# One scan per pair in the state-space stage of a hybrid encoder layer, with norm work moved between ScalarE, GpSimd and VectorE

## The chip, the cores and the metric

The kernel runs on one core of one Trainium2 chip, as one launch. The metric is the device time in microseconds of that launch. Engines are called as in the profile: PE (TensorE), PEld (its weight loads), DVE (VectorE), ACT (ScalarE), POOL (GpSimd), SP (the queue that issues the transfers).

## The reference

One layer of a streaming encoder on 2048 prompt frames with 16 meta tokens in front and on 64 frames of a running stream, width 1024, all in FP32:

```python
z = rmsnorm(h, norm1_g) @ w_in                      # q (8 heads), k, v (2 heads), u (32 groups x 16 channels)
attn = windowed attention over 16 meta keys, the two chunks before and the own chunk, with a sink per head
# state-space model, per group g of 16 channels one complex diagonal state of 64:
bu = einsum(u, bb)                                  # bb, a from A, log_dt, B
x[t] = a * x[t-1] + bu[t]                           # x[-1] = 0 for the prompt, the cached state for the stream
y = Re(C x) + D u
zs = gelu(y);  s_out = zs * sigmoid(zs @ w_glu + b_glu)
h = h + concat(rmsnorm(attn), rmsnorm(s_out)) @ w_out
f = rmsnorm(h, norm2_g) @ w_up                      # 1024 -> 4096
h = h + square(relu(f)) @ w_down
```

Outputs are the frames of prompt and stream, the newest keys and values, and the last state (real and imaginary part) of prompt and stream.

## The kernel before

The 2128 frames are kept with channels in the rows. Matmuls of projections split each FP32 operand into a high and a low part (`xh`, `xl`; a cast on ACT, a difference on DVE) and add three products. The program runs in stages that overlap at their borders.

1. Input projection of u (`u_mm`, L825) and the preparation of the state-space tables on POOL; then the projections of q, k, v (L920) with the attention, chunk by chunk, the tables and maps of the state-space model beside them (`tables`, `store_g`, `store_k`), stored to `reca` and `recb` in DRAM.
2. The state-space stage. The 32 groups are taken as 16 pairs of groups. Frames are taken in 266 chunks of 8 (the last 8 chunks, from `PCH` = 258 on, are the stream's), so the recurrence over chunks has 266 steps. `ssm_step` runs for each pair: `ssm_in` (L1245) makes the input of the recurrence by a matmul, with real and imaginary part in the two halves of the rows and the two groups in two blocks; `ssm_align` (ACT, L1254) copies it so that the two groups lie in the two halves of the rows and the parts in two blocks; `ssm_mix` on DVE turns it by the phase tables (L1264 to L1268), scans (L1272), turns it back (L1276, L1277) and writes the states into `H` (L1282, L1285) with the parts in the rows again; `ssm_out` (L1294, L1295) makes y by two matmuls per group; `ssm_done` and `ssm_write` store it. `r8` holds one decay per row, `g0` the turned initial state. Two small copies take the last states into `fin` (L1287) and set the stream's initial state in `H` (L1288). Between the pairs stand the output projection's attention half (`out`, L1454, its sum on DVE in L1496) and the norms of the attention (`norm_square` to `norm_split`, one block of 352 frames at a time).
3. The GLU (`glu_mm`, L1672), the rest of the output projection into `hd` in DRAM, in six blocks of 352 frames; for the first two blocks the sums of squares for the MLP's norm are collected as the blocks come (`h_squares`).
4. The MLP in three blocks of 704 frames. Up and down projection are done by a seven-product scheme on 2 x 2 blocks (`product`, L1973; `unit`, L2068). Its left operands are combinations of four quarters of the normed frames: for the first block they are made by `x0_load`, `x0_gain`, `x0_sub`, `x0_cut` during the last two blocks of the output projection and after it; the products come in the order `ORD` = 1, 5, 6, 3, 7, 2, 4. The space of operands other than 1 and 6 is only free once the output projection is through.

A Newton step refines each reciprocal root that ACT makes as exp(-ln(v)/2) (`newton`, called by `rsqrt` and by the norms).

All instructions go through `Order.arrange`, a list scheduler written in the kernel: it estimates a length for each instruction, follows the dependences through tiles, pools and DRAM, ranks instructions by the longest way to the end, and fixes one order per engine. Any edit thus draws up every engine's order anew. Each engine and each queue then works in its order.

## Time and profile before

| | us |
|---|---|
| three runs, median (lowest to highest) | 2102.73 (2100.11 to 2104.24) |
| the profiled execution | 2103.09 |
| its span (first to last instruction) | 2100.5 |
| PE busy | 2003.0 (95%) |
| DVE busy | 1800.0 (86%) |
| ACT busy | 1221.7 (58%) |
| POOL busy | 397.0 (19%) |

The span is what the profiler sees between the first and the last instruction; the time of a run is a little longer. Busy time counts an engine's own instructions, overlaps once. The mean granted TensorE clock over the span was 0.984 of full speed.

### The profile page before, as it was taken

What the parts mean: (1) busy time and instruction counts of PE and PEld (TensorE: products, weight loads), DVE (VectorE), ACT (ScalarE), POOL (GpSimd) and SP (SyncE); (2) the same over time, 40 slices, a digit from 0 to 9 for tenths busy, and PEclk for the clock granted to TensorE, in tenths of its full rate; (3) what the DMA queues carried; (4) which work ended last, traced back from release to release, by engine and by line L of the source; (5) the groups of instructions that cost most, each with busy time, mean ns of one, the idle gap of its engine ahead of it and who ended that gap; (6) DMA issues with size and microseconds to landing.
All of it is one profiled execution on the core that took longest, in us unless ns stands there. A gap on an engine that the chain in (4) does not pass through costs nothing.

```text
span 2100.5 us, 34600 instructions
## 1 busy us (share of the span) xinstructions
PE 2003.0 (95%) x12100; PEld 1931.1 (92%) x12100; DVE 1800.0 (86%) x3315; ACT 1221.7 (58%) x2496; POOL 397.0 (19%) x525
## 2 busy tenths in 40 slices
PE   8989999997789988999999999999999999999999
PEld 8987888786679977999999999999999999999999
DVE  8958996679977778999999998789978977887778
ACT  6447677743255545655555666665656655566554
POOL 7954311000002052333233301000000100000000
PEclk9999999999899998999999999999999999999999
DMA  6532332467664385654666676556745764444432
GB/s 224 153 63 76 98 97 72 146 210 239 205 209 127 118 263 189 212 181 165 226 215 201 210 249 220 160 150 207 224 140 152 240 200 141 137 135 138 138 121 96
DMA packets 308335, 354.41 MB, mean 169 GB/s; under 512 B 28865, under 2 KB 220992, under 8 KB 307650
## 3 DMA queue, kind: packets, MB, share of 16 engines
q1 hardware_dynamic: 308018, 352.21, 53.8%
q8 instruction: 95, 1.56, 0.3%
q14 instruction: 78, 0.64, 0.1%
q10 hardware_dynamic: 144, 0.00, 0.0%
HBM read 260.15 MB, written 94.07 MB: 169 GB/s over the span
## 4 chain that ended last, share of the span: by engine, by line
PE 67%; DVE 19%; ACT 5%; DMA 5%; issue 3%; SPq 0%; POOL 0%; DVEq 0%; ACTq 0%; POOLq 0%
PE psd L2068 28%; PE bB L1973 10%; PE bA L1973 10%; PE bC L1973 8%; PE pso L1454 3%; PE psqkv L920 3%; PE psg L1672 2%; DMA hd<-xo 1%; PE pu L825 1%; DVE ul L1963 1%; DVE ab L1272 1%; DVE ss L799 1%; PE pv L1185 1%; DVE wl L2037 1%; DVE acc L2077 1%
## 5 line engine op out<-in xcount | busy, mean ns | idle before, releaser
L2068 PE MATMUL psd<-hh,wh 128*128 128x352 f32 x1344 | 433.8, 323 | 3.8 <-DVE acc L2077 2.9
L2068 PE MATMUL psd<-hl,wh 128*128 128x352 f32 x1344 | 432.0, 321 | 2.0 <-DVE hl L2056 2.0
L2068 PE MATMUL psd<-hh,wl 128*128 128x352 f32 x1344 | 430.6, 321 | 0.0
L2077 DVE TENSOR_TENSOR acc<-psd,acc 128x352 f32<-128x352 f32 x624 | 313.2, 514 | 36.5 <-PE psd L2068 35.7
L2068 PEld LDWEIGHTS psd<-hh,wh 128*128 128x128 f32 x1344 | 252.0, 188 | 6.2 <-DVE acc L2077 3.8
L2068 PEld LDWEIGHTS psd<-hl,wh 128*128 128x128 f32 x1344 | 252.7, 188 | 2.7 <-DVE hl L2056 2.6
L2068 PEld LDWEIGHTS psd<-hh,wl 128*128 128x128 f32 x1344 | 252.3, 188 | 0.0
L1962 ACT CAST uh<-ur 128x512 fp32r<-128x512 f32 x144 | 89.3, 620 | 151.3 <-PE bB L1973 64.0
L2037 DVE TENSOR_TENSOR wl<-d,wh 128x512 fp32r<-128x512 f32 x240 | 175.2, 730 | 0.3 <-ACT wh L2036 0.2
L2036 ACT CAST wh<-d 128x512 fp32r<-128x512 f32 x240 | 146.5, 617 | 34.1 <-PE psd L2068 28.3
L1973 PE MATMUL bA<-xl,uh 128*128 128x352 f32 x480 | 155.9, 325 | 5.4 <-DVE xl L1791 5.4
L1973 PE MATMUL bA<-xh,uh 128*128 128x352 f32 x480 | 157.6, 328 | 3.0 <-ACT xh L1790 1.6
L1962 ACT CAST uh<-us 128x512 fp32r<-128x512 f32 x128 | 79.4, 621 | 133.5 <-PE bB L1973 68.5
L1973 PE MATMUL bB<-xh,uh 128*128 128x352 f32 x480 | 156.0, 325 | 0.0
L1973 PE MATMUL bA<-xh,ul 128*128 128x352 f32 x480 | 155.9, 325 | 0.0
L1973 PE MATMUL bB<-xh,ul 128*128 128x352 f32 x480 | 155.4, 324 | 0.0
L1973 PE MATMUL bB<-xl,uh 128*128 128x352 f32 x480 | 154.8, 323 | 0.0
L920 PE MATMUL psqkv<-wqa,xh 128*128 128x384 f32 (+1 forms) x544 | 138.3, 348 | 7.0 <-ACT z L933 6.7
L1973 PE MATMUL bC<-xl,uh 128*128 128x352 f32 x384 | 125.4, 327 | 5.6 <-DVE xl L1791 5.6
L2056 DVE TENSOR_TENSOR hl<-hid,hh 128x352 fp32r<-128x352 f32 x240 | 129.2, 538 | 1.1 <-ACT hh L2055 1.1
L1963 DVE TENSOR_TENSOR ul<-ur,uh 128x512 fp32r<-128x512 f32 x144 | 108.7, 755 | 24.6 <-ACT uh L1962 24.6
L1973 PE MATMUL bC<-xh,ul 128*128 128x352 f32 x384 | 125.2, 326 | 2.3 <-DVE ul L1963 2.2
(446 smaller groups left out, 5295.7 us busy)
## 6 DMA issues: line engine op xcount, KB each, us to landing
ur<-in_w_up_dram SPq DMA_DIRECT2D x160, 256.0 KB
d<-in_w_down_dram SPq DMA_DIRECT2D x128, 256.0 KB
us<-usd SPq DMA_DIRECT2D x128, 256.0 KB
d<-dsd SPq DMA_DIRECT2D x96, 256.0 KB
hd<-xo SPq DMA_DIRECT2D x48, 352.0 KB
usd<-s SPq DMA_DIRECT2D x64, 256.0 KB
dsd<-d SPq DMA_DIRECT2D x48, 256.0 KB
dx<-in_w_down_dram SPq DMA_DIRECT2D x48, 256.0 KB
```

Of the source, the lines that this page charges most:

```text
L799: nc.vector.tensor_reduce(out=ss[b], in_=x.rearrange("p k n -> p n k"), axis=AX.X, op=ALU.add)
L920: nc.tensor.matmul(t["ps"][c][:n, :384], x, w[k][:, c * 384 : c * 384 + 384], start=(k == 0 and i == 0), stop=(k == KT - 1 and i == 2))
L1454: nc.tensor.matmul(ps, w, x, start=(i == 0), stop=(i == len(seq) - 1))
L1672: nc.tensor.matmul(ps, w[:, k, m * P : (m + 1) * P], x[:, k], start=(k == 0 and i == 0), stop=(k == 3 and i == 2))
L1962: nc.scalar.copy(h, src)
L1963: nc.vector.tensor_sub(l, src, f32(h))
L1973: nc.tensor.matmul(ps, w[:, k], x[:, k], start=(p in BANK and k == 0 and a == 0), stop=False, skip_group_check=True)
L2036: nc.scalar.copy(h, src)
L2037: (e if p in POOLED[i >= NPR] else v).tensor_sub(l, src, f32(h))
L2056: eng.tensor_sub(l, src, f32(h))
L2068: nc.tensor.matmul(ps, w[:, c], y, start=(p in DFIRST and n == 0), stop=False, skip_group_check=True)
L2077: v.tensor_add(ACC[eh, nh][:, x], ps, ACC[eh, nh][:, x])
```

## The change

It edits four things.

1. State-space stage. The scan of a pair is one instruction over both parts and over prompt and stream: its multiplier is a tile `dk` that ACT makes from a mask `dm` (ones, with zeros where a recurrence begins) and the decay, and the stream's turned initial state is added to its first step beforehand. `H` keeps the layout of the scan, groups in the rows and parts in the blocks, so two sums over all rows replace four over half the rows, and each of the two state matmuls of a pair becomes two over 64 rows; `recb` is stored to match. The small copies go from DVE to ACT. The last states are put in the output's order once, at the end (`ssm_last`).
2. `newton` makes the square of y on ACT first and is then two DVE operations instead of three.
3. The variance of the attention's, GLU's and MLP's norms (a scale and a shift of a PSUM row) goes from DVE to ACT.
4. From POOL to DVE: the sums of squares of the first two blocks, the products with the norm's root in `gain`, the differences in `x0_sub`, and the low part of operand 2 (`x0_rest`).

```diff
 def newton(y, v, t, eng):
-    eng.scalar_tensor_tensor(out=t, in0=v, scalar=-0.5, in1=y, op0=ALU.mult, op1=ALU.mult)
-    eng.tensor_mul(t, t, y)
+    nc.scalar.activation(t, y, AF.Square)
+    eng.scalar_tensor_tensor(out=t, in0=v, scalar=-0.5, in1=t, op0=ALU.mult, op1=ALU.mult)
     eng.scalar_tensor_tensor(out=y, in0=t, scalar=1.5, in1=y, op0=ALU.add, op1=ALU.mult)
...
             for c, t in enumerate((vr, vi)):
-                for gg in range(2):
-                    r = slice(64 * gg, 64 * gg + 64)
-                    nc.sync.dma_start(recb[js, 64 * c : 64 * c + 64, gg * P : (gg + 1) * P].rearrange("j p (d c) -> p j d c", c=16),
-                                      t[r, :, 1:9, :])
+                nc.sync.dma_start(recb[js, :, c * P : (c + 1) * P].rearrange("j p (d c) -> p j d c", c=16), t[:, :, 1:9, :])
...
-        elif i in (2, 3):
-            c = i - 2
-            for lo, hi, init in ((0, PCH, 0.0), (PCH, NCH, g0[:, c, j : j + 1])):
-                v.tensor_tensor_scan(out=x["ab"][:, c, lo:hi], data0=r8[:, j : j + 1].broadcast_to((P, hi - lo)),
-                                     data1=x["ab"][:, c, lo:hi], initial=init, op0=ALU.mult, op1=ALU.add)
+        elif i == 2:
+            x["dk"] = wide("dk")
+            nc.scalar.activation(x["dk"], Sx["dm"], AF.Copy, scale=r8[:, j : j + 1])
+            ab = x["ab"][:, :, PCH]
+            v.scalar_tensor_tensor(out=ab, in0=g0[:, :, j], scalar=r8[:, j : j + 1], in1=ab, op0=ALU.mult, op1=ALU.add)
+        elif i == 3:
+            fl = lambda a: a.rearrange("p c n -> p (c n)")
+            v.tensor_tensor_scan(out=fl(x["ab"]), data0=fl(x["dk"]), data1=fl(x["ab"]), initial=0.0, op0=ALU.mult, op1=ALU.add)
...
             H = x["H"] = GH[j % 2]
-            for gg in range(2):
-                r = slice(64 * gg, 64 * gg + 64)
-                v.tensor_sub(H[0:64, gg, 1:], x["p1"][r, 0], x["p2"][r, 1])
-            for gg in range(2):
-                r = slice(64 * gg, 64 * gg + 64)
-                v.tensor_add(H[64:, gg, 1:], x["p1"][r, 1], x["p2"][r, 0])
-            gs = slice(2 * j, 2 * j + 2)
-            v.tensor_copy(Sx["fin"][:, :, gs].rearrange("p q g -> p g q"), H[:, :, PCH : NCH + 1 : NCH - PCH])
-            v.tensor_copy(H[:, :, PCH], Sx["h0"][:, gs])
+            v.tensor_sub(H[:, 0, 1:], x["p1"][:, 0], x["p2"][:, 1])
+            v.tensor_add(H[:, 1, 1:], x["p1"][:, 1], x["p2"][:, 0])
+            nc.scalar.copy(Sx["fin"][:, :, :, j].rearrange("p q c -> p c q"), H[:, :, PCH : NCH + 1 : NCH - PCH])
+            nc.scalar.copy(H[:, :, PCH], Sx["h0"][:, :, j])
+
+    def ssm_last():
+        for c in range(2):
+            for gg in range(2):
+                nc.scalar.copy(Sx["st"][64 * c : 64 * c + 64, :, gg::2], Sx["fin"][64 * gg : 64 * gg + 64, :, c])
+        nc.sync.dma_start(O["st"], Sx["st"])
...
-            nc.tensor.matmul(y[:, gg, :NCH], x["rb"][:, gg * P : gg * P + P], x["H"][:, gg, 0:NCH], start=False, stop=True)
+            r = slice(64 * gg, 64 * gg + 64)
+            for c in range(2):
+                nc.tensor.matmul(y[:, gg, :NCH], x["rb"][r, c * P : c * P + P], x["H"][r, c, 0:NCH], start=False, stop=(c == 1))
...
-        nc.vector.tensor_scalar(out=v, in0=ps, scalar1=1.0 / 512, scalar2=EPS, op0=ALU.mult, op1=ALU.add)
+        nc.scalar.activation(v, ps, AF.Copy, scale=1.0 / 512, bias=EPS)
...
-                nc.gpsimd.tensor_add(HS[n], HS[n], sq[:, i])
+                nc.vector.tensor_add(HS[n], HS[n], sq[:, i])
...
-            nc.gpsimd.tensor_mul(x, x, M["rs"][:, nh].unsqueeze(1).broadcast_to((P, 2, OB)))
+            nc.vector.tensor_mul(x, x, M["rs"][:, nh].unsqueeze(1).broadcast_to((P, 2, OB)))
...
-        nc.vector.tensor_scalar(out=var, in0=ps, scalar1=1.0 / D, scalar2=EPS, op0=ALU.mult, op1=ALU.add)
+        nc.scalar.activation(var, ps, AF.Copy, scale=1.0 / D, bias=EPS)
...
-    out_block(NOB - 1, {0: (lambda: x0_sub("d", "b", "a", e), lambda: u_get(0, (0, 0), (1, 0))),
+    out_block(NOB - 1, {0: (lambda: x0_sub("d", "b", "a", v), lambda: u_get(0, (0, 0), (1, 0))),
...
-                        2: (lambda: x0_sub("b", "c", "b", e),), 3: (lambda: x0_sub("a", "c", "d", v),),
+                        2: (lambda: x0_sub("b", "c", "b", v),), 3: (lambda: x0_sub("a", "c", "d", v),),
...
-            x0_cut(2, "d", e)
+            x0_cut(2, "d", v)
```

What this makes of the engines' orders is shown at three places. First DVE in the middle of the state-space stage, one pair (`o` and `p` are the turned input and output, `ab` the scan's tile; scans read as SCALAR_TENSOR_TENSOR here). Before:

```order
L1267 TENSOR_TENSOR ab<-o_5589,o_5590 128x266
L1410 TENSOR_TENSOR ss<-sq 128x352
L1268 TENSOR_TENSOR ab<-o_5589,o_5590 128x266
L1282 TENSOR_TENSOR H_5195<-p_5594,p_5595 64x266 x2
L1285 TENSOR_TENSOR H_5195<-p_5594,p_5595 64x266 x2
L1272 SCALAR_TENSOR_TENSOR ab<-r_90,ab 128x258
L1287 COPY fin<-H_5195 128x2x2
L1272 SCALAR_TENSOR_TENSOR ab<-r_90,g_89,ab 128x8
L1288 COPY H_5195<-h_5190 128x2
L1272 SCALAR_TENSOR_TENSOR ab<-r_90,ab 128x258
L1272 SCALAR_TENSOR_TENSOR ab<-r_90,g_89,ab 128x8
```

These are ten operations on states and scan (two rows stand for two each). With the change the same place reads:

```order
L1269 TENSOR_TENSOR ab<-o_5586,o_5587 128x266
L1287 TENSOR_TENSOR H_5192<-p_5591,p_5592 128x266
L1288 TENSOR_TENSOR H_5192<-p_5591,p_5592 128x266
L1270 TENSOR_TENSOR ab<-o_5586,o_5587 128x266
L1507 TENSOR_TENSOR xo<-pso,xo 128x352
L1276 SCALAR_TENSOR_TENSOR ab<-g_89,r_90,ab 128x2
L1266 TENSOR_TENSOR o_5655<-RI,ra 128x532
L1279 SCALAR_TENSOR_TENSOR ab<-dk,ab 128x532
```

The ten operations became four (the sum `xo` of a projection and the first turn of the next pair now stand between them).

Then PE at the same place, from one pair's output to the next pair's input (`psy` the output y, `pss` the recurrence's input, `pso` the output projection). Before:

```order
L1294 MATMUL psy<-U,rb 128x266
L1245 MATMUL pss<-U,ra 128x266
L1295 MATMUL psy<-H_5195,rb 128x266
L1294 MATMUL psy<-U,rb 128x266
L1295 MATMUL psy<-H_5195,rb 128x266
```

Each group has one matmul on the states. With the change:

```order
L1303 MATMUL psy<-U,rb 128x266
L1306 MATMUL psy<-H_5190,rb 128x266 x2
L1303 MATMUL psy<-U,rb 128x266
L1306 MATMUL psy<-H_5190,rb 128x266 x2
L1247 MATMUL pss<-U,ra 128x266 x2
```

Each matmul on the states is there twice, over half the rows, and the full-row matmuls stand around each two of them.

Last, DVE from the last sums of the output projection to the MLP's first operands (`xa` to `xd` the four quarters of the normed frames, `rs` the norm's root, `xl` a low part). Before:

```order
L421 SCALAR_TENSOR_TENSOR rs<-ms,rs 128x352
L1496 TENSOR_TENSOR xo<-pso,xo 128x352 x3
L1791 TENSOR_TENSOR xl_8020<-xa,xh_8019 128x704
L1496 TENSOR_TENSOR xo<-pso,xo 128x352 x3
L1791 TENSOR_TENSOR xl_8020<-xa,xh_8019 128x704
L1496 TENSOR_TENSOR xo<-pso,xo 128x352
L1809 TENSOR_TENSOR xa<-xc,xd 128x704
L1791 TENSOR_TENSOR xl_8176<-xd,xh_8175 128x704
```

Only low parts and one pair of differences are DVE's here. With the change:

```order
L1820 TENSOR_TENSOR xd<-xb,xa 128x704
L1507 TENSOR_TENSOR xo<-pso,xo 128x352 x3
L1802 TENSOR_TENSOR xl_8021<-xa,xh_8020 128x704
L1793 TENSOR_TENSOR xc<-xc,rs 128x704 x2
L1820 TENSOR_TENSOR xb<-xc,xb 128x704 x2
L1974 TENSOR_TENSOR ul<-s,uh 128x512
L1820 TENSOR_TENSOR xa<-xc,xd 128x704
L1507 TENSOR_TENSOR xo<-pso,xo 128x352 x3
L1820 TENSOR_TENSOR xa<-xc,xd 128x704
L1802 TENSOR_TENSOR xl_8107<-xa,xh_8106 128x704
L1802 TENSOR_TENSOR xl_8177<-xd,xh_8176 128x704
```

The products with `rs` and the differences, which stood on POOL, now stand on DVE among the sums of the last projections. On PE the twelve matmuls of the first MLP product, which came after the last projection, now stand among the last 60 matmuls of it.

## Rows read from the trace of the kernel before

**Rows 1.** The page: busy us, share of the span, instructions.

```profile
PE 2003.0 (95%) x12100; PEld 1931.1 (92%) x12100; DVE 1800.0 (86%) x3315; ACT 1221.7 (58%) x2496; POOL 397.0 (19%) x525
```

**Rows 2.** Busy time by stretch: start:end, length, engines (instructions), granted clock, DMA share, GB/s.

```profile
455.00:590.00 135.00, 103.16 (x466) 84.75 (x467) 130.15 (x302) 44.61 (x94) 0.00 (x0) 0.91 0.73 234
640.00:740.00 100.00, 99.98 (x612) 98.34 (x611) 74.69 (x120) 53.04 (x86) 18.44 (x16) 1.00 0.44 132
767.00:830.00 63.00, 46.69 (x223) 41.76 (x223) 50.85 (x64) 31.44 (x60) 24.94 (x14) 0.81 0.58 191
1225.00:2075.00 850.00, 850.00 (x5322) 849.58 (x5321) 710.80 (x1382) 515.67 (x1041) 29.99 (x21) 1.00 0.54 168
```

**Rows 3.** Groups by line, PE, 455 to 590 us: instructions, busy us, mean ns, idle before.

```profile
L1454 PE MATMUL pso<-xh,zt 128*128 128x352 f32 x182 | 52.9, 357 | 0.5 <-ACT xh L1437 0.5
L1454 PE MATMUL pso<-xl,zt 128*128 128x352 f32 x92 | 32.3, 351 | 3.4 <-DVE xl L1438 3.4
...
L1295 PE MATMUL psy<-H,rb 128*128 128x266 f32 x60 | 21.5, 444 | 8.9 <-DVE H L1288 8.9
L1245 PE MATMUL pss<-U,ra 128*128 128x266 f32 x64 | 20.5, 439 | 16.4 <-DMA ra<-reca 14.5 <-DMA U<-ud 1.7 <-issue 0.2
```

**Rows 4.** Timeline of PE in the state-space stage: start us, us, instruction.

```profile
483.38 0.61 PE L1294 MATMUL psy<-U,rb 128*128 128x266 f32 x2
483.83 0.61 PE L1295 MATMUL psy<-H,rb 128*128 128x266 f32 x2
```

**Rows 5.** Groups by line, DVE, 455 to 590 us.

```profile
L1272 DVE TENSOR_TENSOR_SCAN ab<-r,ab 128x258 f32<-128x258 f32 x32 | 22.1, 690 | 0.4
L1282 DVE TENSOR_TENSOR H<-p,p 64x266 f32<-64x266 f32 x32 | 13.6, 424 | 0.6 <-PE psy L1295 0.4
...
L1272 DVE TENSOR_TENSOR_SCAN ab<-r,g,ab 128x8 f32<-128x8 f32 x32 | 6.9, 216 | 0.1
...
L1438 DVE TENSOR_TENSOR xl<-x,xh 128x704 fp32r<-128x704 f32 x6 | 5.3, 881 | 0.0
...
L1288 DVE COPY H<-h 128x2 f32<-128x2 f32 x15 | 2.3, 156 | 0.0
...
L1417 DVE TENSOR_SCALAR v<-psr 128x352 f32<-128x352 f32 x3 | 1.6, 517 | 0.0
```

**Rows 6.** Timeline of DVE in the state-space stage.

```profile
480.67 0.70 DVE L1272 TENSOR_TENSOR_SCAN ab<-r,ab 128x258 f32<-128x258 f32 x1
...
482.28 0.70 DVE L1264 TENSOR_TENSOR o<-RI,ra 128x532 f32<-128x532 f32 x1
```

**Rows 7.** Groups by line, whole span: the score matmuls on 128 and on 70 rows.

```profile
L1168 PE MATMUL s<-QT,KB 128*128 128x256 f32 x62 | 21.3, 348 | 2.9 <-ACT e L1176 2.3 <-DVE KB L1019 0.6
...
L1168 PE MATMUL s<-QS,KS 70*128 70x256 f32 x62 | 19.5, 323 | 1.9 <-DVE QS L1156 1.9
```

**Rows 8.** Timeline of PE where a 32-column operand follows a full one.

```profile
246.95 0.51 PE L920 MATMUL psqkv<-wqa,xl 128*128 128x384 f32 x2
247.39 0.41 PE L636 MATMUL pm<-vr,bd 128*32 128x128 f32 x2
```

**Rows 9.** Groups by line: POOL and DVE, 740 to 805 us; PE, 767 to 805 us.

```profile
L1809 POOL TENSOR_TENSOR xd<-xb,xa 128x704 f32<-128x704 f32 x2 | 4.0, 2023 | 0.0
...
L1791 DVE TENSOR_TENSOR xl<-xc,xh 128x704 fp32r<-128x704 f32 x2 | 3.2, 1622 | 0.0
L1791 DVE TENSOR_TENSOR xl<-xd,xh 128x704 fp32r<-128x704 f32 x2 | 3.2, 1616 | 0.0
L1809 DVE TENSOR_TENSOR xa<-xc,xd 128x704 f32<-128x704 f32 x2 | 2.9, 1426 | 0.0
...
L1973 PE MATMUL bA<-xl,uh 128*128 128x352 f32 x13 | 5.9, 454 | 5.4 <-DVE xl L1791 5.4
...
L1973 PE MATMUL bC<-xl,uh 128*128 128x352 f32 x8 | 3.9, 491 | 5.6 <-DVE xl L1791 5.6
```

More of the change, by code (lines that the diff above doesn't have):

```diff
@@ L1220, in ssm_open @@
         Sx["sp"] = ssp.enter_context(pool("sp", 1, "right"))
-        h0 = Sx["h0"] = Sx["sp"].tile([P, G], F32, name="h0")
-        nc.sync.dma_start(h0, I["h0"])
-        Sx["fin"] = Sx["sp"].tile([P, 2, G], F32, name="fin")
+        h0 = Sx["h0"] = Sx["sp"].tile([P, 2, PAIRS], F32, name="h0")
+        nc.sync.dma_start(h0, I["par"][:, 3:5])
+        dm = Sx["dm"] = Sx["sp"].tile([P, 2, NCH], F32, name="dm")
+        nc.gpsimd.memset(dm, 1.0)
+        nc.gpsimd.memset(dm[:, :, 0], 0.0)
+        nc.gpsimd.memset(dm[:, :, PCH], 0.0)
+        Sx["fin"] = Sx["sp"].tile([P, 2, 2, PAIRS], F32, name="fin")
+        Sx["st"] = Sx["sp"].tile([P, 2, G], F32, name="st")
         for i in range(2):
@@ L1625, in tile_trunk @@
     z_load(3)
-    nc.sync.dma_start(O["st"], Sx["fin"])
+    ssm_last()
     pys.close()
@@ L1647, in h_squares @@
             HS[n] = WO["na"].tile([P, OB], F32, tag=f"hs{n}", name="hs", bufs=1)
-            nc.gpsimd.tensor_add(HS[n], sq[:, 0], sq[:, 1])
+            nc.vector.tensor_add(HS[n], sq[:, 0], sq[:, 1])
         else:
             for i in range(2):
-                nc.gpsimd.tensor_add(HS[n], HS[n], sq[:, i])
+                nc.vector.tensor_add(HS[n], HS[n], sq[:, i])
     def glu_split(n, ks):
```

## The prediction

> **What bounds the kernel now.** I read the busy shares first [rows 1]: PE has work for 95% of the span, so most of this kernel is bound by matmuls, and an edit elsewhere pays only where PE waits. The busy time by stretch [rows 2] shows where that is. From 1225 to 2075 us PE is busy without a break, and its 5322 records give the pitch of a matmul of 352 columns at full clock: 850 / 5322 = 0.160 us. From 640 to 740 us it is full too. Two stretches differ. In the state-space stage, 455 to 590 us, PE is busy 103.16 of 135 us at a mean granted clock of 0.91, while DVE is busy 130.15 us: DVE is the bound. At the start of the MLP, 767 to 830 us, PE is busy 46.69 of 63 us at a clock of 0.81, DVE 50.85 us and POOL 24.94 us. The edits that matter fall into these two.
>
> What PE's work there would take at full clock is needed below. In the first stretch its 466 records are 182 + 92 = 274 output-projection matmuls [rows 3] and 192 others, nearly all halves of the FP32 matmuls of the state-space model (each such matmul leaves two records). Two halves follow two halves after 483.83 - 483.38 = 0.45 us [rows 4], 0.225 us each. So 274 x 0.160 + 192 x 0.225 = 43.8 + 43.2 = 87.0 us. In the second, 223 x 0.160 = 35.7 us of work stand in 63 us: 27.3 us are lost to waits and to the lower of the two clock levels (1.2 against 2.4 GHz).
>
> **State-space stage, what DVE sheds.** In each of 16 pairs the four scans go, two of 258 and two of 8 elements (0.690 and 0.216 us [rows 5]), with the two small copies between them: by their starts 482.28 - 480.67 = 1.61 us [rows 6]. The four 64-row sums into H go too, 4 x 0.424 = 1.70 us [rows 5]. In comes one scan of 532 elements. By the two lengths shown a scan costs (0.690 - 0.216) / 250 = 1.90 ns per element, so 0.216 + 524 x 0.0019 = 1.21 us. It reads a whole tensor as multiplier where the old one read one number per row, which no row shows; I take the old rate, as the nearest. Its ends: 0.5 us less per pair at the rate of the sums (0.424 us for 266 elements [rows 5]), 1.0 us more, 16 us in all, if the second stream doubles the old rate. Further come one two-element operation at 0.16 us, as the small copy, and two sums of 266 elements over all rows at no more than 0.42 us each, as the 64-row ones [rows 5]: 2.21 us in all. Net 1.61 + 1.70 - 2.21 = 1.10 us per pair, 17.6 us over 16.
>
> Three norms in this stage also lose the variance and one product of Newton's step to ACT: 3 x 2 x 0.517 [rows 5] = 3.1 us. DVE falls from 130.15 to about 109.5 us. The multiplier tile, the two small copies and Newton's square land on ACT: about 16 x 1.1 and 3 x 1 us, an estimate from DVE's small copy and from 532 elements at a bit over 1 ns each. ACT is busy 44.61 of 135 us [rows 2], so 65 us leave it free. The copy of the initial state now stands between H and the matmul that reads it, on another engine; where PE has no projection to run meanwhile that is some 0.4 us per pair, inside the allowance below.
>
> **State-space stage, what PE gains.** H now holds the real part in one block and the imaginary part in the other, the two groups in the two halves of the rows. So each of 32 matmuls on 128 rows becomes two on 64. Fewer rows do not shorten a matmul: the score matmul on 70 rows takes 0.323 us, the one on 128 rows 0.348 us [rows 7]. So 64 more halves at 0.225 us come on top: 14.4 us. With them come changes between full and 64-row operands, four per pair, 64 in all. No row shows that; nearest is the change to a 32-column operand: two matmuls of 384 columns (0.160 x 384 / 352 = 0.175 us each) begin at 246.95 us, and the next, of the other shape, at 247.39 instead of 247.30 [rows 8]: 0.1 us. 64 x 0.1 = 6.4 us. PE then needs 87.0 + 14.4 + 6.4 = 107.8 us, nearly the same as DVE.
>
> The Trainium skill (TensorEngine Tiling (Array Packing), Key Properties) says that a change of tiling mode drains TensorE, and also that different tiles may execute in parallel. The latter finds no use here: in the new order two neighbouring 64-row matmuls read the same rows. What the former would do is rival A.
>
> So the stage holds 109.5 us of DVE's and 107.8 us of PE's work, each in its own in-order queue. I add the 4.85 us for which DVE idles now (135 - 130.15 [rows 2]; the stage begins with a wait for tables, and PE waits 14.5 us for them in all [rows 3]), and 3 us because two full engines wait for each other at times, a third of what PE now waits for H, 8.9 us [rows 3]. That is 117 us, **18 us less**. Some projections that no longer fit into the stage run after it, in place of waits for transfers; I cost that at nothing, and 1 to 2 us if those waits are gone.
>
> **Start of the MLP.** Ten operations on the first operands (six products with the norm's root, four differences) and two low parts go from POOL to DVE. One takes 2.02 us on POOL [rows 9] and 0.88 us on DVE where POOL rests, as the low part of the same shape in [rows 5]. Beside a busy POOL, DVE's own operations of that shape take 1.62, 1.62 and 1.43 us on average, twice each [rows 9]: 2 x (0.74 + 0.74 + 0.55) = 4.1 us lost by these alone. So DVE takes on 12 x 0.88 = 10.6 us and gets back 4 to 8. What changes is the order: the products and differences now stand ahead of the last projections, where PE is busy, and POOL's serial chain (12 x 2 = 24 us) is off the path. PE's waits for a low part of x, 5.4 + 5.6 us [rows 9], mostly go. Late next are the two operands whose frames are loaded only once the last projections have freed their space: 4 us of wait are left for them. With a busier PE part of the low clock goes too: it hides up to 0.19 x 63 = 12 us [rows 2], I take 3. 11 - 4 + 3 = **10 us less**. Ends: 6 us worse (10.6 - 4, nothing hidden) to 22 us better (27.3 less a first wait of 5).
>
> **The rest.** Newton's squares, variances and 14 sums of squares (POOL to DVE) elsewhere lie beside a PE that is full (its second and last row) [rows 2] or, in the attention stage, are small: 1 us less in all, with 3 us either way, since every engine's order is drawn up anew. The states' rows and their one store at the stage's end are a few small copies, hidden by projections.
>
> Sum: 18 + 10 + 1 = 29 us. The profiled execution took 2103.1 us (span 2100.5, 2.6 around it), 0.4 above the median shown. 2103 - 29 = **2074 us**.
>
> **Rivals.**
> A. *The change of shape drains PE.* A drained change costs at most a matmul's length less its pitch, 0.444 - 0.225 = 0.22 us [rows 3, 4], and a weight load that is no longer hidden, 84.75 / 467 = 0.18 us [rows 2]: 0.40 us. 64 x 0.40 = 25.6 us put PE at 127 us and the stage, with 5 us of waits, at 132: 3 us gained, 2089 us. The page named above states the drain, without a price. For it: PE would be the bound at once. Against it: the 0.1 us of [rows 8]. Chance 0.13.
> B. *The MLP's start gains nothing.* DVE has 50.85 us of work in 63 and takes more into its in-order queue, where the sums of the projections wait behind it, and PE for their buffers. Then 18 + 1 us are left: 2084 us. Against it: the stretched rows. Chance 0.17.
> C. *Slower.* The drains of A keep the granted clock at its lower level through the stage, and a change costs twice as much, 0.8 us: PE needs 101.4 + 64 x 0.8 = 153 us, the stage with 5 us of waits 158. That is 23 us lost, 11 gained elsewhere: 2115 us. It decides from 0.68 us per change: 101.4 + 43.5 + 5 = 150 us, which eats the other 11 us and 4 more. Against it: the price is far above the one row there is. Chance 0.04.
> D. *A and B together*: 3 + 0 + 1 us, 2099 us. Chance 0.04.
>
> **Numbers.** The forecast has 0.62, with a range of its own from 2060 (24 + 16 + 3 less) to 2086 (12 + 5). The range to hold 8 times in 10 takes in A, B and the far ends: from 2057 (22 + 22 + 2 less) to 2091 (6 + 4 + 2). A measurement of this kernel tells about 0.2%, 4 us, from no change. Faster by more: the forecast, A and B, 0.92; within it: D, 0.04; slower: C, 0.04.
>
> **What would show it.** Right, if the state-space stage takes about 117 us, with one scan of 1.2 us per pair, DVE and PE both busy over 90% of it, the granted clock near 1 and 64-row halves at 0.225 us; and if the first MLP products stand among the last projections, with no wait of PE for a low part over 2 us. Wrong, if at each change of rows a matmul comes 0.4 us late (A), if the scan's rate is not 1.9 ns, if PE waits for the sums of the last projections (B), or if DVE waits for ACT's copies of the next pair, which I cost at nothing because in the new order they serve a pair three later.

## The result, and the profile after

| | before | after |
|---|---|---|
| median of the runs timed side by side, us (lowest to highest) | 2103.48 (2100.11 to 2105.42) | 2068.68 (2065.12 to 2071.01) |
| ratio, 95% interval | | 0.9835 (0.9822 to 0.9848) |
| span of the profiled execution, us | 2100.5 | 2067.8 |
| PE, DVE, ACT, POOL busy, us | [rows 1] | 2007.6, 1761.2, 1258.5, 355.3 |

34.8 us less; 2074 was forecast, in a range from 2057 to 2091. The sum is nearly right, but not all of its parts are. I cut both executions at the same five points of the program: the first matmul of the state-space stage (`pss`), the last matmul of y (`psy`), the last GLU matmul (`psg`), the first sum of a unit of the MLP (`acc` from `sa`) and the last sum. First the busy time by stretch of the kernel before, cut so (start:end, length, busy us and instructions of PE, PEld, DVE, ACT and POOL, granted clock, DMA share, GB/s):

```profile
0.00:456.10 456.10, 420.12 (x2514) 380.31 (x2515) 369.57 (x632) 285.93 (x652) 182.18 (x393) 0.99 0.42 120
456.10:593.50 137.40, 105.95 (x478) 86.79 (x479) 133.57 (x311) 44.61 (x94) 0.00 (x0) 0.91 0.72 229
593.50:729.30 135.80, 132.27 (x805) 129.43 (x804) 98.43 (x154) 82.84 (x124) 15.86 (x14) 1.00 0.47 146
729.30:828.80 99.50, 82.58 (x439) 76.39 (x438) 77.86 (x105) 48.82 (x90) 41.57 (x24) 0.88 0.70 225
828.80:2096.70 1267.90, 1262.06 (x7870) 1258.13 (x7868) 1120.07 (x2115) 759.54 (x1537) 157.43 (x94) 1.00 0.56 178
```

The same view of the changed kernel:

```profile
0.00:446.90 446.90, 415.43 (x2511) 381.55 (x2511) 359.41 (x604) 294.21 (x681) 175.93 (x396) 0.98 0.42 120
446.90:565.90 119.00, 117.22 (x535) 87.33 (x535) 109.81 (x208) 66.33 (x156) 0.00 (x0) 1.00 0.86 277
565.90:706.20 140.30, 136.96 (x831) 133.80 (x830) 97.22 (x159) 86.39 (x131) 0.00 (x0) 1.00 0.45 143
706.20:795.50 89.30, 76.83 (x425) 72.23 (x424) 72.67 (x108) 50.84 (x97) 25.82 (x12) 0.92 0.76 240
795.50:2064.00 1268.50, 1261.17 (x7868) 1257.76 (x7867) 1121.59 (x2107) 760.74 (x1545) 153.53 (x94) 1.00 0.56 178
```

Read the lengths line by line. Attention and all ahead of it: 9.2 us less, which the forecast did not have. State-space stage: 18.4 less (forecast 18). GLU stage: 4.5 more. Start of the MLP: 10.2 less (forecast 10). The rest: 0.6 more. Together 32.7 us of the span. The GLU stage did not get worse: it has 26 more PE records than before, and 26 x 0.160 (the pitch of a matmul in the prediction) is 4.2 us. The start of the MLP has 14 fewer, and the state-space stage has 57 more where 64 halves were added, 7 fewer projections. So projections have moved into the GLU stage from both sides (a few records can be missing, so the counts are good to some five).

What the state-space stage is made of now, DVE's groups by line and PE's, 447 to 566 us: instructions, busy us, mean ns, idle before.

```profile
L1279 DVE TENSOR_TENSOR_SCAN ab<-dk,ab 128x532 f32<-128x532 f32 x16 | 20.1, 1256 | 0.1
L1287 DVE TENSOR_TENSOR H<-p,p 128x266 f32<-128x266 f32 x16 | 6.8, 426 | 0.0
L1276 DVE SCALAR_TENSOR_TENSOR ab<-g,r,ab 128x2 f32<-128x2 f32 x16 | 3.4, 212 | 0.0
```

```profile
L1306 PE MATMUL psy<-H,rb 64*128 64x266 f32 x128 | 38.3, 414 | 0.0
L1303 PE MATMUL psy<-U,rb 128*128 128x266 f32 x64 | 20.7, 405 | 0.0
L1247 PE MATMUL pss<-U,ra 128*128 128x266 f32 x64 | 18.3, 408 | 2.2 <-DMA ra<-reca 2.2
```

The scan takes 1.256 us (1.21 forecast): with a second tensor as multiplier the rate is nearly the old one, (1.256 - 0.216) / 524 = 1.98 ns per element beside 1.90, with 0.216 us for 8 elements [rows 5]. A sum over all rows takes 0.426 us, as the 64-row ones did [rows 5]. PE waits for nothing in the stage but tables, 2.2 us: the wait for H of [rows 3] is gone, and PE is the bound, busy 117.22 of 119.0 us at full clock. Its timeline over one pair (start us, us, instruction):

```profile
460.75 0.61 PE L1303 MATMUL psy<-U,rb 128*128 128x266 f32 x2
461.29 1.16 PE L1306 MATMUL psy<-H,rb 64*128 64x266 f32 x4
462.39 0.71 PE L1303 MATMUL psy<-U,rb 128*128 128x266 f32 x2
463.03 1.16 PE L1306 MATMUL psy<-H,rb 64*128 64x266 f32 x4
464.13 1.17 PE L1247 MATMUL pss<-U,ra 128*128 128x266 f32 x4
```

Twelve halves take 464.13 - 460.75 = 3.38 us. At 0.225 us each they would take 2.70, so this pair pays 0.68 us for its four changes between 128 and 64 rows: 0.17 us each, where the forecast took 0.1 and rival A 0.40. (Any difference between a 64-row half and a full one is in this figure.)

### The profile page after: what moved, and what is told of

Read it like the earlier page. It is cut to its first block, busy times and chain, and to the rows that moved or that the text cites. A ratio compares the mean times of both kernels' runs of the same rounds, so it can differ in the third digit from the quotient of the medians.

```text
span 2067.8 us, 34656 instructions
## 1 busy us (share of the span) xinstructions
PE 2007.6 (97%) x12164; PEld 1932.7 (93%) x12164; DVE 1761.2 (85%) x3185; ACT 1258.5 (61%) x2608; POOL 355.3 (17%) x502
## 4 chain that ended last, share of the span: by engine, by line
PE 77%; DVE 12%; ACT 4%; DMA 3%; issue 2%; POOL 1%; SPq 0%; DVEq 0%; ACTq 0%; POOLq 0%
PE psd L2079 29%; PE bA L1984 10%; PE bB L1984 10%; PE bC L1984 8%; PE pso L1465 6%; PE psqkv L917 2%; PE pu L822 2%; PE psy L1306 2%; PE psg L1683 1%; PE pv L1182 1%; DVE acc L2088 1%; PE psy L1303 1%; PE pss L1247 1%; DVE wl L2048 1%; DVE M L1145 1%
## 5 line engine op out<-in xcount | busy, mean ns | idle before, releaser
L1984 PE MATMUL bC<-xh,uh 128*128 128x352 f32 x384 | 125.5, 327 | 6.8 <-ACT uh L1973 5.0
L2003 ACT ACTIVATE hid<-hid 128x352 f32<-128x352 f32 x144 | 71.3, 498 | 90.4 <-DVE hid L2002 85.3
```

What stands on the lines that cost most here:

```text
L1984: nc.tensor.matmul(ps, w[:, k], x[:, k], start=(p in BANK and k == 0 and a == 0), stop=False, skip_group_check=True)
L2003: nc.scalar.activation(h, h, AF.Relu)
```

## The experiments

All runs were timed beside the kernel before on the same chip; ratios are to that, with 95% intervals. Three questions were open: which edit brought the 9 us ahead of the stage, which half of the state-space edit pays, and what now bounds the two stretches that got shorter.

**The three edits one by one.** Each of three kernels is the one before with one group of the change's hunks: item 1 (`s_only`), items 2 and 3 (`n_only`), item 4 (`x_only`). One line of each stands for its group:

```diff
 s_only: all of item 1, as
+            v.tensor_tensor_scan(out=fl(x["ab"]), data0=fl(x["dk"]), data1=fl(x["ab"]), initial=0.0, op0=ALU.mult, op1=ALU.add)
 n_only: newton and the three variances, as
+        nc.scalar.activation(t, y, AF.Square)
 x_only: all of item 4, as
+            nc.vector.tensor_mul(x, x, M["rs"][:, nh].unsqueeze(1).broadcast_to((P, 2, OB)))
```

s_only, expected:

> The kernel before with the edits of the state-space stage alone (one scan, states in the frame's rows, small copies on ACT, recb stores). Theory 1 (the prediction's sums, with the early gain due to the redrawn order or to the norms): the state-space stage falls from 137.5 us to about 121, 2103 - 17 = 2086 us, and its first matmul (pss) stays within 3 us of 456 us. Theory 2 (the early gain of 9 us comes from the two recb stores per part that replace four): pss begins near 447 us and the time is about 2077. Theory 3 (the gain is DVE's relief by the norms, the scan hardly matters): stage over 130 us, 2095 or more.

n_only, expected:

> The kernel before with Newton's squares and the variances on ACT alone. Theory 1: 3 us in the state-space stage (DVE's bound there) and 1 elsewhere, 2099 us; pss within 3 us of 456. Theory 2 (DVE's relief in the attention is what gained 9 us ahead of the state-space stage): pss begins near 447 us, 2091 us. Theory 3 (early gain is the order drawn up anew): pss anywhere between 446 and 466, and PE's waits for the softmax and the sums change places without a change of DVE's busy time.

x_only, expected:

> The kernel before with the moves from POOL to DVE alone (sums of squares, products with the root, differences, one low part). Theory 1: 10 us at the start of the MLP and nothing ahead of it, 2093 us; from the last GLU matmul to the first sum of the units 99.6 us now, 89 then. Theory 2 (rival B: DVE in order holds the sums of the projections): 2101 or more, with PE waiting for the sums. Theory 3 (part of the 4 us lost in the GLU stage comes with this move, by the sums of squares that stand in DVE's queue): 6 us net, 2097, with the GLU stage 4 us longer.

Measured:

| kernel | median, us | ratio (interval) | up to `pss` | state space | GLU | MLP start | rest |
|---|---|---|---|---|---|---|---|
| before, profiled | | | 456.1 | 137.4 | 135.8 | 99.5 | 1267.9 |
| s_only | 2084.41 | 0.9896 (0.9880 to 0.9912) | 459.2 | 123.8 | 130.4 | 99.0 | 1266.4 |
| n_only | 2099.42 | 0.9976 (0.9967 to 0.9984) | 450.8 | 135.2 | 139.5 | 98.4 | 1270.7 |
| x_only | 2094.90 | 0.9951 (0.9938 to 0.9965) | 456.8 | 136.9 | 135.9 | 91.0 | 1267.3 |

The three ratios multiply to 0.9824, within the interval of the whole change: the edits hardly touch each other. The state-space hunks bring 13.6 + 5.4 = 19.0 us in the state-space and GLU stages together and nothing ahead of them, so the recb stores (theory 2) are out and theory 1 is right in kind, with a stage 3 us longer than its 121 and part of the gain in the GLU stage. The moves from POOL bring 8.5 us at the MLP's start alone, theory 1. n_only comes to the 2099 us of theory 1, but not in its places: 5.3 us go ahead of the state-space stage, which lies between theories 1 and 2, 2.2 in it and 1.1 at the MLP's start, and 3.7 + 2.8 come back in the GLU stage and the rest.

**Is the early gain DVE's relief, or luck of a new order?** Every edit makes the list scheduler draw up all orders anew. Two kernels bear on this: the kernel before with only a planner constant changed, and the changed kernel with the old Newton step.

```diff
 redrawn (on the kernel before)
-            dur[k] = self.cost(i, e, ws, rs, dma[k]) * (1.04 if e in ("DVE", "Pool", "Activation") else 1)
+            dur[k] = self.cost(i, e, ws, rs, dma[k]) * (1.06 if e in ("DVE", "Pool", "Activation") else 1)
 newton_undone (on the changed kernel)
-        nc.scalar.activation(t, y, AF.Square)
-        eng.scalar_tensor_tensor(out=t, in0=v, scalar=-0.5, in1=t, op0=ALU.mult, op1=ALU.mult)
+        eng.scalar_tensor_tensor(out=t, in0=v, scalar=-0.5, in1=y, op0=ALU.mult, op1=ALU.mult)
+        eng.tensor_mul(t, t, y)
```

redrawn, expected:

> The kernel before with no work changed: only the list scheduler's factor on the estimated lengths of DVE, POOL and ACT instructions goes from 1.04 to 1.06, so that every engine's order is drawn up anew. Theory 1 (a new order by itself costs or gains little, and the early gain of the changed kernel is DVE's relief): the time within 3 us of before, 2102 to 2108, and the first matmul of the state-space stage within 2 us of 456. Theory 2 (the early gain is luck of the order): that matmul begins anywhere from 447 to 465, and the time moves by 4 us or more.

newton_undone, expected:

> The changed kernel with Newton's step as before (three DVE operations, no square on ACT). Theory 1 (DVE's relief in the attention shortens it): DVE's busy time up to the state-space stage rises by 8 to 10 us, its first matmul comes 5 us later, at 452 us, and little is lost in the stage itself, where PE is full: 2074 us. Theory 2 (the order): that matmul within 2 us of 447 and 2067 to 2070 us, or a shift that no DVE time answers to. Theory 3 (the prediction's sum for the norms in the stage, 3 us, and nothing in the attention): 447 us, 2072.

The redrawn kernel took 2104.13 us, ratio 0.9998 (0.9989 to 1.0007), its theory 1. newton_undone took 2076.23, ratio 0.9863 (0.9850 to 0.9877), theory 1 too. The ratio of the changed kernel is 0.9835 (0.9822 to 0.9848), so undoing the step costs 0.0028 of the time, 5.9 us; the two intervals just miss each other. (The medians differ by 7.6 us, but they come from different series.) The busy time by stretch up to `pss`, of redrawn and then of newton_undone:

```profile
0.00:455.90 455.90, 416.56 (x2515) 379.72 (x2515) 375.03 (x632) 287.24 (x652) 178.12 (x393) 0.99 0.42 118
```

```profile
0.00:454.10 454.10, 417.09 (x2511) 379.24 (x2512) 368.12 (x630) 287.09 (x655) 181.72 (x396) 0.99 0.43 120
```

This one new order leaves `pss` where it was, 455.9 us. The old Newton step puts 368.12 - 359.41 = 8.7 us back on DVE and moves `pss` 7.2 us later, while PE's work is the same (2511 records) and PE stands idle 37.0 us up to `pss` instead of 31.5. By the ratios the step is worth 5.9 us undone, and 5.0 us added to the kernel before together with the variances (n_only), in two different orders. So the whole times show that the Newton step pays, some 5 us, with wide limits. The rows of it, DVE's groups up to `pss` in the kernel before, then DVE's and ACT's in the changed kernel:

```profile
L419 DVE SCALAR_TENSOR_TENSOR tt<-v,y 128x10 f32<-128x10 f32 x16 | 3.6, 228 | 1.4 <-ACT y L1041 1.1
L420 DVE TENSOR_TENSOR tt<-tt,y 128x10 f32<-128x10 f32 x16 | 5.7, 354 | 0.2
L421 DVE SCALAR_TENSOR_TENSOR y<-tt,y 128x10 f32<-128x10 f32 x16 | 2.8, 176 | 0.3
```

```profile
L420 DVE SCALAR_TENSOR_TENSOR tt<-v,tt 128x10 f32<-128x10 f32 x16 | 4.4, 272 | 2.0 <-ACT tt L419 1.8
L421 DVE SCALAR_TENSOR_TENSOR y<-tt,y 128x10 f32<-128x10 f32 x16 | 3.2, 202 | 0.2
```

```profile
L419 ACT ACTIVATE tt<-y 128x10 f32<-128x10 f32 x16 | 3.3, 208 | 0.2
```

The chain of one step hardly shortens, 0.228 + 0.354 + 0.176 = 0.76 us before, 0.208 + 0.272 + 0.202 = 0.68 after. What goes is DVE's time: with the seven steps on 304 columns and the two on 352, DVE's part of all Newton steps up to `pss` falls from 26.0 to 17.2 us. So DVE's relief is the likelier way, though no run separates it from the chain.

A new order can still move `pss` by some us: s_only and tiles_interleaved (below) begin the stage 3 us later than the kernels they are built on, with a few stores changed ahead of it in the one and nothing in the other; state_and_norm_sums (below) begins it 8.5 us earlier than its own base and loses that again in the stage. So a single landmark is good to some 8 us, the 7.2 us of newton_undone alone would not decide, and the whole times do.

**Which half of the state-space edit pays?** scan_alone is the changed kernel with the old H.

```diff
-            v.tensor_sub(H[:, 0, 1:], x["p1"][:, 0], x["p2"][:, 1])
-            v.tensor_add(H[:, 1, 1:], x["p1"][:, 1], x["p2"][:, 0])
+            for gg in range(2):
+                r = slice(64 * gg, 64 * gg + 64)
+                v.tensor_sub(H[0:64, gg, 1:], x["p1"][r, 0], x["p2"][r, 1])
...
-            for c in range(2):
-                nc.tensor.matmul(y[:, gg, :NCH], x["rb"][r, c * P : c * P + P], x["H"][r, c, 0:NCH], start=False, stop=(c == 1))
+            nc.tensor.matmul(y[:, gg, :NCH], x["rb"][:, gg * P : gg * P + P], x["H"][:, gg, 0:NCH], start=False, stop=True)
```

> The changed kernel with H as before (parts in the rows): four sums over 64 rows per pair on DVE, two matmuls of 128 rows per group, the old recb stores; the one scan and the copies on ACT stay. Theory 1 (the stage is set by the fuller of DVE and PE): DVE's work rises from 110 by 16 x 0.85 = 13.6 to 123.4 us, PE's falls from 117 by 16 x (4 x 0.225 + 0.68) = 25 to about 92 us; the stage takes about 128 us instead of 119, 2077 us. Theory 2 (PE's doubled matmuls cost what DVE's relief gives): the stage stays within 3 us of 119, 2067 to 2071. Theory 3 (the 64-row matmuls are a loss): stage under 115, 2064 or less.

It took 2086.82 us, ratio 0.9914 (0.9900 to 0.9927): theory 1 in direction, 10 us beyond its number. State-space and GLU stage of this kernel:

```profile
450.30:585.90 135.60, 112.23 (x527) 91.89 (x528) 131.58 (x250) 74.34 (x157) 0.00 (x0) 0.95 0.77 244
585.90:721.10 135.20, 129.77 (x772) 125.96 (x771) 91.23 (x149) 77.94 (x125) 0.00 (x0) 0.99 0.44 141
```

DVE is the bound again, 131.58 of 135.60 us, and PE's clock has a dip again. The two stages together take 270.8 us against 259.3, 11.5 more (the state-space stage took in 56 projections that stand in the GLU stage otherwise, hence its 16.6 and the GLU's -5.1); 3.4 us more stand ahead of `pss`, where the two kernels differ in four stores per part instead of two and in the order. n_only and x_only multiply to 0.9927, so the one scan with its small copies on ACT brings 0.0013, under 3 us and within the intervals of nothing; the other 17 or so come from H. The title of the change names the scan, but the layout that the scan left in place, and that spares two half-empty sums per pair, is what pays.

**The changes of shape, and two groups side by side.** tiles_interleaved is the changed kernel with the matmuls of y in another order: a pair's two full matmuls come first, then its four 64-row ones, upper and lower half of the rows in turn.

```diff
             nc.tensor.matmul(y[:, gg, :NCH], x["rb"][:, (2 + gg) * P : (3 + gg) * P], x["U"][:, gg], start=True, stop=False)
-            r = slice(64 * gg, 64 * gg + 64)
-            for c in range(2):
+        for c in range(2):
+            for gg in range(2):
+                r = slice(64 * gg, 64 * gg + 64)
                 nc.tensor.matmul(y[:, gg, :NCH], x["rb"][r, c * P : c * P + P], x["H"][r, c, 0:NCH], start=False, stop=(c == 1))
```

> The changed kernel, with the matmuls of y of a pair in another order: both over 128 rows first, then the four over 64 rows, with the two groups (upper and lower half of the rows) taking turns: two changes of shape per pair instead of four. Theory 1 (a change costs 0.17 us, tiles run one after the other): PE's work falls by 32 x 0.17 = 5 us in a stage that PE bounds, 2063 us. Theory 2 (neighbouring matmuls on different rows run side by side): the four 64-row matmuls of a pair take about 1.0 us where they now take 2 x 1.1 = 2.2, PE's work falls by up to 19 us, DVE's 111 us then bound the stage at about 113, 2061 or less. Theory 3 (only the first change after a pair matters, or the order hardly helps): within 2 us of the changed kernel, 2067 to 2069.

PE's timeline over one pair of it:

```profile
490.05 1.17 PE L1303 MATMUL psy<-U,rb 128*128 128x266 f32 x4 [0.24 <-ACT ys L1312]
491.14 1.17 PE L1307 MATMUL psy<-H,rb 64*128 64x266 f32 x8
492.24 0.94 PE L1247 MATMUL pss<-U,ra 128*128 128x266 f32 x3
```

Eight 64-row halves take 492.24 - 491.14 = 1.10 us, as long as four did in the changed kernel. Neighbouring matmuls on different halves of the rows run side by side, which the Trainium skill says of different tiles (TensorEngine Tiling (Array Packing), Key Properties) and this trace now shows. This pair takes 2.19 us of PE instead of 3.38; over the stage PE's busy time falls by 117.22 - 102.73 = 14.5 us. Yet the kernel took 2069.03 us, ratio 0.9826 (0.9814 to 0.9839), the same as the changed kernel: theory 2 in its mechanism and nearly in the stage (113 us), theory 3 in the time. The stage is shorter by 4.6 us only:

```profile
449.70:564.10 114.40, 102.73 (x532) 79.87 (x533) 109.33 (x207) 65.12 (x153) 0.00 (x0) 0.99 0.83 274
```

DVE is busy 109.33 of 114.40 us: the bound has gone back to it, and PE's time to spare stands as waits (5.3 us for ACT's copy `ys`, 2.3 for H, 3.5 for others at the stage's matmuls, 2.5 for a low part at a projection). And `pss` begins 2.8 us later, at 449.7, and the MLP's start and what follows take 2.5 us more. Those I put down to the new order; no run shows it for them.

**DVE relieved further.** state_on_act builds on it: the stream's initial state is multiplied by the decay once for all pairs, on POOL, and ACT adds it to one column of `RI`; the two-element operation on DVE goes, and `dk` has two buffers. state_and_norm_sums also lets PE sum the norms' squares.

```diff
+        for c in range(2):
+            t = RI[:, c, PCH : PCH + 1]
+            nc.scalar.activation(t, t, AF.Identity, bias=ah[:, c, j : j + 1], scale=1.0)
...
-            ab = x["ab"][:, :, PCH]
-            v.scalar_tensor_tensor(out=ab, in0=g0[:, :, j], scalar=r8[:, j : j + 1], in1=ab, op0=ALU.mult, op1=ALU.add)
... (state_and_norm_sums)
+            for k in range(4):
+                nc.tensor.matmul(ps, ones, sq[:, k], start=(k == 0), stop=(k == 3))
```

state_on_act, expected:

> tiles_interleaved, with the stream's initial state brought in another way: its product with the decay is made once for all pairs, early on POOL (six small operations), and ACT adds it to the one column of RI (two operations of one element per pair) ahead of the rotation. That takes from DVE the two-element operation of each pair (16 x 0.21 = 3.4 us in the state-space stage) and 48 small ones in the attention stage, where the turned state was made; the multiplier tile dk gets a second buffer, so that ACT's copies don't queue behind its wait for the scan. Theory 1 (with the two groups side by side PE has time to spare in the stage, and DVE is its bound again): stage from 114.4 to 111 us, the attention stage 2 to 4 us shorter by DVE's relief, 2063 us. Theory 2 (ACT's copies in front of the rotation are the chain that counts): stage 114 or more, DVE waiting for RI, 2067 to 2071.

state_and_norm_sums, expected:

> state_on_act, and the attention's norms of blocks 2 to 5 sum their squares by four matmuls with ones instead of two DVE sums and one matmul: three norms in the stage, DVE 3 x 1.4 = 4.2 us less, PE 3 x 3 x 0.6 = 5.4 us more. Theory 1 (DVE bounds the stage, PE has 12 us to spare there): 3 to 4 us less than state_on_act. Theory 2 (PE's time comes back in the GLU stage, where PE is full): the stages together within 2 us of state_on_act.

state_on_act took 2070.63 us, ratio 0.9843 (0.9829 to 0.9857), and state_and_norm_sums 2069.30, ratio 0.9834 (0.9821 to 0.9848): both misses of theory 1. The stage of state_on_act:

```profile
450.90:566.60 115.70, 102.65 (x534) 79.96 (x534) 108.40 (x191) 70.10 (x184) 0.00 (x0) 0.99 0.86 281
```

It takes 115.7 us, no less than in tiles_interleaved, although DVE has 16 operations fewer; its busy time fell by 0.9 us only, not by the 3.4 expected. Nor did the 48 small ones fewer ahead of the stage help (`pss` at 450.9 us). What PE, and then ACT, wait for there (us in total, times, longest):

```profile
PE psy L1302 <- ACT ys L1311: 8.2, 8, 2.5
PE pss L1245 <- ACT RI L1254: 1.9, 3, 0.9
```

```profile
ACT dk L1275 <- DVE ab L1278: 16.0, 11, 2.7
ACT fin L1288 <- DVE H L1287: 9.3, 7, 3.1
ACT RI L1254 <- PE pss L1245: 9.0, 2, 6.8
```

ACT, busy 70 of 115.7 us, waits in its queue for DVE before it can make `dk`, and its copies for PE stand behind that. Stage and time are those of theory 2, but its sign, DVE waiting for `RI`, came to 1.2 us only. I read this as the loop from PE through ACT to DVE and back keeping the stage from falling below some 115 us, and not any one engine's work. No run takes the loop apart, and since DVE is busy 108.40 of the 115.7 us, a plain bound on DVE with a few waits is not ruled out. In state_and_norm_sums the stage took 126.0 us with 34 more records, but began 8.5 us earlier than in state_on_act, and up to the last GLU matmul the two are level (708.9 and 709.2 us): its theory 2.

**What is left at the MLP's start.** PE's longest waits of the changed kernel from 706 to 795 us:

```profile
PE bC L1984 <- ACT uh L1973: 5.0, 1, 5.0
PE bC L1984 <- DVE xl L1802: 2.8, 1, 2.8
PE bC L1984 <- ACT xh L1801: 1.8, 1, 1.8
```

The 5.0 us are for a cast of weights, `uh`, on ACT, which reads a sum, `s`, made on POOL. The sums, the cast and the matmul that waits, in the timelines of POOL, ACT and PE:

```profile
769.74 9.58 POOL L1957 TENSOR_TENSOR s<-ur,s 128x512 f32<-128x512 f32 x1 [12.27 <-DVE ul L1974]
779.28 1.26 POOL L1955 TENSOR_TENSOR s<-ur 128x512 f32<-128x512 f32 x1
```

```profile
779.35 0.62 ACT L1973 CAST uh<-s 128x512 fp32r<-128x512 f32 x1 [2.06 <-POOL s L1957]
```

```profile
780.02 0.66 PE L1984 MATMUL bC<-xh,uh 128*128 128x352 f32 x1 [5.01 <-ACT uh L1973]
```

The first of the two sums takes 9.58 us; the other eleven of this shape in the stretch take 1.26 to 1.90. DVE works without a gap until 778.2 us, 14 instructions beside this one, and the sum ends 1.1 us after. Eight later POOL sums of this shape take 2.1 to 5.6 us, and each of them ends 1.22 to 1.24 us after DVE's first instruction with an operand in PSUM, where PE leaves its results; all DVE instructions ahead of that one read two operands from SBUF. One of the eight, and the DVE instruction:

```profile
1024.21 4.85 POOL L1953 TENSOR_TENSOR s<-s,ur 128x512 f32<-128x512 f32 x1 [1.30 <-DVE ul L1974]
1027.82 1.37 DVE L2088 TENSOR_TENSOR acc<-psd,acc 128x352 f32<-128x352 f32 x3
```

(The Trainium skill, SBUF — State Buffer, "SBUF: two separate sides", has it that a DVE instruction with two inputs in SBUF and a POOL instruction that reads SBUF contend for a shared port pair, which whichever starts first holds for its whole instruction, while the other blocks. The nine sums fit this; that a row of such DVE instructions holds POOL off through all of them is more than the Trainium skill says there.)

The slow sum is not the whole of the 5.0 us, though. ACT waited 2.06 us for it; ahead of that, ACT's queue stood on casts of the down weights (`wh`), which wait for a row of sums (`dx`) on DVE. In tiles_interleaved the same two sums take 1.75 and 1.74 us and are done by 771.9 us, and PE waits as long:

```profile
768.46 1.75 POOL L1958 TENSOR_TENSOR s<-ur,s 128x512 f32<-128x512 f32 x1 [12.56 <-DVE hl L2068]
776.11 0.62 ACT L2048 CAST wh<-dx 128x512 fp32r<-128x512 f32 x1 [1.79 <-DVE dx L2039]
777.16 1.14 ACT L1974 CAST uh<-s 128x512 fp32r<-128x512 f32 x2
777.82 0.66 PE L1985 MATMUL bC<-xh,uh 128*128 128x352 f32 x1 [5.06 <-ACT uh L1974]
```

x_only has the slow sum (9.57 us) and a wait of 5.0 us. tiles_and_sums is tiles_interleaved with this row's two sums on DVE.

```diff
-                e.tensor_sub(SW[3], blk(0, 0), blk(1, 0))
+                (v if i == 1 else e).tensor_sub(SW[3], blk(0, 0), blk(1, 0))
-                e.tensor_sub(SW[4], blk(0, 1), SW[2])
+                (v if i == 1 else e).tensor_sub(SW[4], blk(0, 1), SW[2])
```

> The changed kernel with the 64-row matmuls of the two groups taking turns (as in tiles_interleaved), and with two weight sums of the second row (L1957, L1955, for the row with index 1 alone) on DVE instead of POOL. In the changed kernel one of these two takes 9.58 us on POOL beside a DVE that is busy without a break, and PE then waits 5.0 us for the weights made of it. Theory 1 (DVE's work keeps POOL from its operands): that wait goes, DVE takes on 2 x 0.68 us, from the last GLU matmul to the first sum of a unit 86 us instead of 90, 2065 us. Theory 2 (DVE is the bound of that stretch, and the wait is only replaced by another): 89 to 92 us, 2068 to 2070.

It took 2068.42 us, ratio 0.9830 (0.9816 to 0.9843), and the stretch 90.2 us instead of 90.7: theory 2. Since these two sums were not slow in tiles_interleaved, the run cannot tell what a slow one costs. DVE's and then PE's timeline:

```profile
775.65 0.67 DVE L2049 TENSOR_TENSOR wl<-d,wh 128x512 fp32r<-128x512 f32 x1
776.26 0.67 DVE L1956 TENSOR_TENSOR s<-ur 128x512 f32<-128x512 f32 x1
```

```profile
775.83 0.43 PE L1985 MATMUL bB<-xh,uh 128*128 128x352 f32 x1 [3.86 <-ACT uh L1974]
777.58 0.66 PE L1985 MATMUL bB<-xh,ul 128*128 128x352 f32 x1 [1.16 <-DVE ul L1975]
```

The sum now takes 0.67 us, but it stands behind the whole row of sums of the down weights in DVE's queue, at 776.26, and PE waits 3.9 + 1.2 us for weights, about as before. The 3.9 us end before that sum begins: the cast that PE waits for starts at 775.16 us on ACT, again behind the casts of `wh`, which waited 2.55 and 0.42 us for `dx`. So the row of sums on DVE and ACT's queue behind it are the likelier cause of the wait in all three kernels. That an earlier place in either queue would end it was not tried. None of these kernels is faster than the changed one by more than its interval.

## Why the prediction was right, and where not

- **State-space stage, 18 us less: right**, 18.4. DVE's 109.5 us came out at 109.81, the scan at 1.256 instead of 1.21, the two sums as assumed. The copies on ACT and the granted clock, 1.00, are as forecast. DVE waited 1.4 us for ACT's copies, which were costed at nothing. That DVE and PE would come out level was not right: PE was busy 117.22 us, 9.4 more than the 107.8 forecast, and it was the bound. The changes of shape, forecast at 0.1 us each, are 3 to 4.5 us of that: 0.17 us in the pair shown, and 0.15 us over the whole stage, where the 192 halves for `psy` take 52.6 us from start to next start and 192 x 0.225 is 43.2. Most of the rest is that the projections' records in the stage follow each other after 0.178 us on average and not 0.160, 4.8 us over 271 records; no run shows why. The 4.85 and 3 us allowed for DVE's waits covered this by luck: in their place stands PE's work, for PE waits for nothing but tables.
- **"The latter finds no use here"**, of matmuls side by side: true of the order as written, and the order could be changed at no cost (tiles_interleaved). It took 14.5 us off PE's busy time, of which 4.6 reached the stage and nothing the time of the whole kernel.
- **Start of the MLP, 10 us less: right in size**, 10.2, of which x_only shows 8.5; some 2 us are the 14 records that went to the GLU stage. First products do stand among the last projections, the first of them at 733.5 us. The waits for a low part fell from 5.4 + 5.6 [rows 9] to 2.8 + 0.5 us, and the 2.8 us at one place are over the 2 us named. The 4 us for operands loaded late did not come as such (0.5 us for a low part of one of them); in their place came the wait for a cast of weights, 5.0 us, which the forecast did not have.
- **The rest, 1 us less: the term that failed.** "Newton's squares ... in the attention stage, are small": they are 8.7 us of DVE's time, and some 6 us of the kernel's (5.9 by the ratios of newton_undone and the changed kernel, 7.2 at `pss`). The rows to see it were in the trace of before: 16 steps on 10 columns, 7 on 304 and 2 on 352, three operations each, 0.18 to 0.60 us apiece, beside a PE that stood idle 36 of 456.1 us. The prediction took the two stretches with the lowest PE share and priced nothing in this one. The other 2 us of the early gain no run places.
- **The GLU stage, nothing or 1 to 2 us: 4.5 us more**, because projections moved into it. That nearly cancels half of the early gain, and so the total came out 5 us below the forecast and not 9. That is luck, for the forecast had neither in this size.
- **Rivals.** A is out: 0.17 us per change, far from 0.40. B is out: DVE is full for long stretches at the MLP's start, but PE's waits there are not for the projections' sums, and 10 us came. C and D fall with A; the granted clock, which C has at its lower level, was 1.00 in the stage.

## What to carry to other kernels

Count a small edit to a helper at every place that calls it, and price it wherever PE is idle at all, not only where PE is idle most: 25 Newton steps, each some 0.35 us lighter on DVE on average, were about a sixth of this change. Where a layout leaves half-filled vector operations, moving the layout change into a matmul's row halves can pay even if it doubles the matmuls; put those on different row halves next to each other, and they run side by side. And when the bound passes from one engine to the next, expect the second relief to bring a fraction: 14.5 us less of PE's busy time gave the stage 4.6 here, and 16 operations fewer on DVE after that gave nothing. Before moving the work that an engine seems to wait for, look at what stands ahead of it in each queue: the wait for weights stayed where the slow sum was gone.

## What the runs showed of the chip

- Two FP32 matmuls on rows 0 to 63 and 64 to 127, issued next to each other into different blocks of `psy`, run at the same time: 8 halves in 1.10 us, 4 in 1.10 us without a neighbour on the other rows.
- A change between 128 and 64 rows costs about 0.17 us of PE in the pair shown, 0.15 us over the stage, the mean over both directions (with any difference between a 64-row half and a full one in it).
- A scan whose multiplier is a whole tensor costs nearly the same per element as one with a number per row: 1.256 us for 532 elements, 1.98 ns each beside 1.90.
- A POOL sum of 128x512, 1.3 to 1.9 us beside a DVE with gaps, took 9.58 us beside DVE instructions that each read two operands from SBUF. It and eight others that took over 2 us ended 1.1 to 1.24 us after DVE's first gap or first instruction with an operand in PSUM.
